# GpSimd's adaptive-norm sums in two runs around the mixer's last normalisation, its other small front work on VectorE, the second layer's gate in the later stage

## Chip, cores and metric

One NeuronCore of a Trainium2 chip runs the whole computation as one program. The metric is device time in microseconds (us); a run's time is that of one launch, and the number for a kernel is the median of several runs. The engines are named as in the profile: PE is TensorE (matrix products; PEld its weight load), DVE is VectorE, ACT is ScalarE, POOL is GpSimd, SP is SyncE, which here only starts transfers.

## What is computed

512 tokens of width 1024 go through two blocks. The parts that matter here, with the rest left out:

```python
def first_block(x, p, ...):
    h = x
    h = h + mixer(rms_norm(h, g_mix))              # conv of 3 and pooling of 2, 4, 8, 16, between w_in and w_o
    h = h + peer_ffn(rms_norm(h, g_ffn))           # 16 query projections, top 16 of 16384 experts a head
    gate = sigmoid(rms_norm(h, g_ple) @ w_ple_gate)
    h = h + gate * (p @ w_ple_proj)
    return rms_norm(h, g_final)

def second_block(x, c, ctx, c_ctx, ada_w, ada_b, ...):
    for i in range(2):                             # layer 0: window attention; layer 1: latent attention
        shift_x, scale_x, gate_x = split(silu(c) @ ada_w[i] + ada_b[i], 3)
        shift_c, scale_c, gate_c = split(silu(c_ctx) @ ada_w[i] + ada_b[i], 3)
        hx = rms_norm_2(x, norm_g[i]) * (1 + scale_x) + shift_x
        hc = rms_norm_2(ctx, norm_g[i]) * (1 + scale_c) + shift_c
        yx, yc = attention_i(hx, hc)
        x = x + gate_x * yx                        # ctx likewise in layer 0
    return rms_norm_2(x, final_g)
```

The product silu(c) @ ada_w[i] depends on no token. It can be done at any time before the layer that uses it.

## The kernel before

**Stages.** `mix` normalises the four token blocks (128 tokens each), turns them so that features lie on partitions, runs 16 projections of w_in (`proj`) in four groups of four, each with its pooling and its convolution, and then w_o as token-major products: two halves of 512 columns, four token blocks in each. As the second half of a token block is added to `h` (L367), that block's next norm is begun by `Norm.add`. `peer` then turns the normalised blocks (`flip`, L228) and runs 16 queries (`query`, L508 begins the evaluation of each product), each followed by one of 128 chunks of expert_u; after that come the routing (top-k, one-hot products) and the gathers of token block 0, on GpSimd's queue. `ple` computes the gate of the first block, `attn_a` and `attn_b` are the two layers of the second.

**A norm.** `rstat` squares a block on ScalarE (L111, summing along a row), then makes the factor `rn` in two tiny GpSimd operations on 128x1 (L112 and, with a power, L113). VectorE scales the rows with it at L217 (`xs`).

**Weights.** `unit` loads 512 KB (`raw`, three buffers, on SP's queue at L99), ScalarE rounds it into a high part (L93), and VectorE subtracts for the low part (L94, `wl`); each product is three matrix products (L104 to L106). Accumulators are three PSUM tiles (`acc`).

**Adaptive-norm sums.** `Ada.work` is a generator. One step takes 128 rows of ada_w by 512 columns (256 KB), multiplies by one column of `silu_c` per condition (x and context), and adds to `aacc`; eight such steps and one that stores make a half of a third (shift, scale or gate). On GpSimd one step is a load on its own queue (L783), a product (L794; L789 for the first) and a sum (L795) per condition. With `gpsimd=False` the step is one VectorE multiply-add per condition (L797) and a load on SP's queue (L785). Four thirds, (0,0), (0,1), (0,2) and (1,2) as (layer, third), are on GpSimd, (1,0) and (1,1) on VectorE beside `ple` and `attn_a`, where `later` takes two steps a time, 18 times.

**What sets the order.** Each engine executes its own list in order, and waits where an operand isn't there. The lists are made when the program is built: steps of `Ada.work` are drawn by `some(2)` at each projection and after each token block of w_o, then two a query, and a scheduler interleaves them with the rest. `issue_after(k.rs)` lets a load of a step be listed only behind the last norm factor that was written so far.

## Time and profile before

| | us |
|---|---|
| median of 3 runs | 2444.17 (2442.78 to 2445.14) |
| profiled execution | 2457.12 |
| its span | 2455.3 |
| PE busy | 2271.6 (93%) |
| DVE busy | 1858.9 (76%) |
| ACT busy | 1061.2 (43%) |
| POOL busy | 902.5 (37%) |

Busy times are means over stages with different limits, so they are read in stretches. A wait is put down to the operation that came last; the time of waiting in a list shows on the engine that waits, its cause on the engine that it waits for. The profiled execution is one execution, a little longer than the timed ones; durations come from it.

### The profile page before, as it was taken

The page shows a single profiled execution, that of the slowest core. Times are in us where ns is not written, and L with a number is a line of the kernel's source. Part 1 is how long each engine was busy: PE and PEld are TensorE (multiplying, and loading weights), DVE is VectorE, ACT ScalarE, POOL GpSimd, SP SyncE. Part 2 cuts the span into 40 slices and gives each one's busy share as a digit, 9 for nine tenths or more (in the row PEclk, how much of TensorE's full clock was granted, in tenths as well). Part 3 has the DMA queues.
Part 4 walks back from the last instruction along what each step waited for, and adds up shares of the span by engine and source line. Part 5 has one row for each costly group of instructions (what it writes and reads, how often), then busy time and mean ns, then how long its engine had stood idle before and what let it go on. Part 6 is the DMA issues. An engine that isn't in the chain of part 4 may idle for free. (4 is left out here: it accounts for less than half of the span.)

```text
span 2455.3 us, 35344 instructions
## 1 busy us (share of the span) xinstructions
PE 2271.6 (93%) x12631; PEld 1979.8 (81%) x12631; DVE 1858.9 (76%) x3421; ACT 1061.2 (43%) x1855; POOL 902.5 (37%) x1021
## 2 busy tenths in 40 slices
PE   7882999799999899999999999889999989999998
PEld 6661889799999899878888888568888758998886
DVE  8832788999999896888888874783688745378884
ACT  4212333243434343333333344441677623466772
POOL 8998920233232531423233210232233323023331
PEclk9985999899999999999999999999999989999999
DMA  5433543689989989999999975553201042210002
GB/s 192 141 120 104 176 139 123 207 286 335 351 311 356 359 321 333 376 377 388 381 372 364 364 268 160 174 177 105 69 31 34 9 148 89 84 46 27 27 10 95
DMA packets 187215, 492.64 MB, mean 201 GB/s; under 512 B 17294, under 2 KB 70814, under 8 KB 185504
## 3 DMA queue, kind: packets, MB, share of 16 engines
q1 hardware_dynamic: 127056, 265.94, 32.0%
q0 software_dynamic: 49040, 174.12, 19.9%
q10 hardware_dynamic: 10944, 50.34, 5.1%
q8 instruction: 99, 1.62, 0.3%
q14 instruction: 76, 0.62, 0.1%
HBM read 424.78 MB, written 65.55 MB: 200 GB/s over the span
## 5 line engine op out<-in xcount | busy, mean ns | idle before, releaser
L93 ACT ACTIVATE wh<-raw 128x1024 fp32r<-128x1024 f32 (+2 forms) x371 | 387.8, 1049 | 586.0 <-PE acc L105 175.8
L94 DVE TENSOR_TENSOR wl<-raw,wh 128x1024 fp32r<-128x1024 f32 (+2 forms) x371 | 465.4, 1259 | 138.3 <-ACT wh L93 133.0
L435 POOL DMA_INDIRECT grow<-in_expert_r,gidx x128 | 167.4, 1308 | 306.8 <-DVE gdot L448 276.1
L435 POOL DMA_INDIRECT grow<-in_expert_v,gidx x128 | 151.8, 1186 | 347.7 <-DVE h L460 329.8
L448 DVE CUSTOM_DVE_ANT_0 gjunk<-grow,gx 128x1024 bf16<-128x1024 f32 x128 | 156.0, 1219 | 17.2 <-DMA grow<-in_expert_r,gidx 16.7
L460 DVE SCALAR_TENSOR_TENSOR h<-grow,gdot,h 128x1024 f32<-128x1024 f32 x128 | 163.7, 1279 | 0.4
L945 DVE TENSOR_TENSOR ptl<-acc,pth 128x512 fp32r<-128x512 f32 x184 | 123.7, 686 | 30.2 <-ACT pth L944 28.6
L944 ACT ACTIVATE pth<-acc 128x512 fp32r<-128x512 f32 x184 | 106.2, 596 | 51.2 <-PE acc L1475 31.5
L1110 POOL TENSOR_SCALAR p<-p,st 128x256 f32<-128x256 f32 (+2 forms) x96 | 64.6, 674 | 136.9 <-DVE st L1109 97.9
L228 PE MATMUL tr<-ident,xs 128*128 128x128 f32 x220 | 46.3, 339 | 69.3 <-DVE xs L217 56.3
L1456 POOL TENSOR_SCALAR p<-p,st 128x768 f32<-128x768 f32 x64 | 60.3, 942 | 127.3 <-DVE st L1455 104.7
L228 PEld LDWEIGHTS tr<-ident,xs 128*128 128x128 f32 x220 | 32.4, 172 | 83.2 <-issue 31.2
L651 ACT ACTIVATE hs<-acc 128x384 f32<-128x384 f32 x128 | 61.3, 479 | 87.9 <-PE acc L106 87.4
L712 DVE TENSOR_TENSOR pr<-ht,gt 128x384 f32<-128x384 f32 x128 | 70.9, 557 | 15.5 <-DMA ht<-Hd 12.0
L106 PE MATMUL acc<-xn_0h,wl 128*128 128x384 f32 (+2 forms) x175 | 61.6, 352 | 19.7 <-DVE wl L94 19.7
L795 POOL TENSOR_TENSOR aacc<-aacc,araw 128x512 f32<-128x512 f32 x56 | 77.0, 1374 | 1.3
L620 PE MATMUL g<-oh,oh 128*128 128x128 f16 x768 | 56.8, 227 | 20.0 <-ACT gs L622 10.6
L1108 ACT ACTIVATE p<-S,st 128x257 f32<-128x257 f32 (+2 forms) x96 | 62.8, 655 | 25.8 <-DVE st L1106 14.7
L217 DVE TENSOR_SCALAR xs<-h,rn 128x1024 f32<-128x1024 f32 x16 | 12.5, 783 | 79.2 <-POOL rn L113 78.9
L620 PEld LDWEIGHTS <-oh 128*128 128x128 f16 x768 | 47.5, 101 | 29.1 <-issue 18.1
L104 PE MATMUL acc<-xn_0h,wh 128*128 128x384 f32 (+2 forms) x175 | 65.4, 374 | 4.2 <-DVE y L356 4.0
L613 DVE TENSOR_TENSOR oh<-oh,gb 128x1024 f16<-128x1024 f16 x96 | 61.8, 683 | 7.5 <-PE g L620 7.5
(1150 smaller groups left out, 7788.9 us busy)
## 6 DMA issues: line engine op xcount, KB each, us to landing
raw<-in_expert_u SPq DMA_DIRECT2D x128, 512.0 KB, 5.3
raw<-in_expert_v SPq DMA_DIRECT2D x128, 512.0 KB, 7.7
Hd<-hs ACTq DMA_DIRECT2D x64, 384.0 KB, 6.0
Gd<-gs ACTq DMA_DIRECT2D x12, 2048.0 KB, 11.6
gt<-Gd SPq DMA_DIRECT2D x32, 768.0 KB, 8.1
ht<-Hd SPq DMA_DIRECT2D x64, 384.0 KB, 8.8
araw<-in_ada_w POOLq DMA_DIRECT2D x64, 256.0 KB, 3.3
raw<-in_w_in SPq DMA_DIRECT2D x16, 512.0 KB, 3.5
```

What stands on the lines that cost most here:

```text
L93: nc.scalar.activation(hi[:, s], src[:, s], AF.Copy)
L94: self.wl = (sub or nc.vector).tensor_tensor(lo[:, s], src[:, s], hi[:, s].bitcast(F32), OP.subtract).ins
L104: mm(out, a[0], b[0], start=start, stop=False)
L228: k.nc.tensor.transpose(ps[:, i * P : (i + 1) * P], x[:, kc * P : (kc + 1) * P], k.ident)
L435: self.k.nc.gpsimd.indirect_dma_start(t, None, table, at)
L448: nc.vector.tensor_tensor_reduce(junk, t, self.x, 1.0, 0.0, OP.mult, OP.add, self.dot[:, s : s + 1])
L460: nc.vector.scalar_tensor_tensor(self.h, t, self.dot[:, s : s + 1], self.h, OP.mult, OP.add)
L620: nc.tensor.matmul(g[:, i], oh[2][at], oh[q][at], start=q == 0, stop=q == 1)
L712: nc.vector.tensor_tensor(by_g(pr), by_g(cur["h"][:, c % 2]), cur["g"][:, :, c % GC], OP.mult)
L795: nc.gpsimd.tensor_tensor(a, a, t, OP.add)
L944: k.nc.scalar.activation(hi, src, AF.Copy)
L945: (eng or k.nc.vector).tensor_tensor(lo, src, hi.bitcast(F32), OP.subtract)
```

## The change

GpSimd's thirds become (0,0), (0,1), (0,2). Their 54 steps are drawn in two runs. The first: each projection draws one or two steps in turn, 24 in all, and w_o draws none. Its loads may be listed once `mark` is written, a copy of one column of the first norm's last `xs`. The second run's 30 steps multiply by `silu_c2`, a copy of `silu_c` that VectorE makes behind the last L217 of the mixer (`resume`); two of them are drawn at each query. The third (1,2) goes to VectorE, and `later` takes three steps a time. The zeroing of the margins of `u` and `z`, two casts of the pooling's weights (L308, L309) and the four casts of indices in the routing (`sif`) go from GpSimd to VectorE. In the kernel after, lines stand one lower behind L72 (L112 becomes L113), L308 to L356 and L367 keep their numbers, and from `Ada` on they stand eight lower (L795 becomes L803).

```diff
@@ -71,6 +71,7 @@
         self.colt = col
         self.mhalf = self.cp.tile([P, 8], F32, name="mhalf")
         nc.gpsimd.memset(self.mhalf, -0.5)
+        self.mark = self.cp.tile([P, 1], F32, name="mark")
 
     def acc(self):
 
@@ -110,7 +111,7 @@
         nc = self.nc
         nc.scalar.activation(junk[:, :width], src, AF.Square, accum_out=out)
         nc.gpsimd.tensor_scalar(out, out, 1.0 / width, EPS, OP.mult, OP.add)
-        self.rs = nc.gpsimd.tensor_tensor(out, out, self.mhalf[:, :1], OP.pow).ins
+        nc.gpsimd.tensor_tensor(out, out, self.mhalf[:, :1], OP.pow)
 
     def norm_T(self, srcs, width, evac, bufs=5):
 
@@ -214,7 +215,7 @@
             src = x
             junk = sp.tile([P, w], BF16, tag="junk", name=k.nm("junk"), bufs=1)
         k.rstat(src, w, c, junk)
-        k.nc.vector.tensor_scalar(x, src, c, None, OP.mult)
+        k.normed = k.nc.vector.tensor_scalar(x, src, c, None, OP.mult).ins
         return x
 
     def flip(self, xs, evac):
@@ -276,7 +277,7 @@
     return [(src[first + i], kcs) for i in range(count)]
 
 
-def mix(k, h, x, ahead, work):
+def mix(k, h, x, ahead, ada, work):
 
 
     tc, nc, ap = k.tc, k.nc, k.ap
@@ -286,15 +287,14 @@
         mp = es.enter_context(tc.tile_pool(name="mx", bufs=1))
         yf = Feat(k, mp, 8, [(0, TB)], "my")
         unit = k.unit(ap["w_in"][12])
-        norm.flip([norm.add(t) for t in h], k.evac_gain(x, lambda kc: k.col("g_mix", kc)))
-
-        def some(n):
-            for _ in range(n):
-                next(work, None)
+        hn = [norm.add(t) for t in h]
+        k.begun = nc.gpsimd.tensor_copy(k.mark, hn[-1][:, 0:1]).ins
+        norm.flip(hn, k.evac_gain(x, lambda kc: k.col("g_mix", kc)))
 
         def proj(nb):
             uh, ul = unit if nb == 12 else k.unit(ap["w_in"][nb])
-            some(2)
+            for _ in range(1 + nb % 2):
+                next(work)
             return now(k.fm(x, 8, uh, ul, [0]))
 
         for g in range(4):
@@ -305,11 +305,11 @@
             if g == 0:
                 pwh, pwl = k.unit(ap["pool_w"], 512)
                 pwr = hilo(k, mp, [P, 512], "pwr")
-                nc.gpsimd.tensor_copy(pwr[0], pwh[:, 0:512].bitcast(F32))
-                nc.gpsimd.tensor_copy(pwr[1], pwl[:, 0:512].bitcast(F32))
+                nc.vector.tensor_copy(pwr[0], pwh[:, 0:512].bitcast(F32))
+                nc.vector.tensor_copy(pwr[1], pwl[:, 0:512].bitcast(F32))
                 pwh, pwl = pwr
-            nc.gpsimd.memset(u[:, :PAD], 0.0)
-            nc.gpsimd.memset(u[:, PAD + T :], 0.0)
+            nc.vector.memset(u[:, :PAD], 0.0)
+            nc.vector.memset(u[:, PAD + T :], 0.0)
             nc.scalar.activation(u[:, PAD : PAD + T], ps, AF.Copy)
             cur, lo, hi, s = u, 0, T + 2 * PAD, 1
             first = True
@@ -345,8 +345,8 @@
             nc.scalar.activation(c, psc, AF.Copy)
             psv = proj(8 + g)
             z = mp.tile([P, T + 2], F32, tag="z", name=k.nm("z"), bufs=2)
-            nc.gpsimd.memset(z[:, 0:1], 0.0)
-            nc.gpsimd.memset(z[:, T + 1 : T + 2], 0.0)
+            nc.vector.memset(z[:, 0:1], 0.0)
+            nc.vector.memset(z[:, T + 1 : T + 2], 0.0)
             nc.vector.tensor_tensor(z[:, 1 : T + 1], c, psv, OP.mult)
             y = mp.tile([P, T], F32, tag="y", name=k.nm("y"), bufs=2)
             nc.vector.tensor_scalar(y, z[:, 0:T], k.col("conv_w", g), None, OP.mult)
@@ -370,7 +370,8 @@
 
         ahead()
         units = [tm_units(ap["w_o"], 4 * nh, 2, 4) for nh in range(2)]
-        k.tm(yf, 8, units, range(TB), evac, between=8 * [lambda: some(2)])
+        k.tm(yf, 8, units, range(TB), evac)
+        ada.resume()
 
     return flips(k, norm, xs, x, "g_ffn"), xs
 
@@ -528,7 +529,7 @@
 
     def routing(tb):
         sif = rp.tile([P, 16, 16], BF16, tag="sif", name=k.nm("sif"), bufs=2)
-        nc.gpsimd.tensor_copy(sif, si[:, tb])
+        nc.vector.tensor_copy(sif, si[:, tb])
         cand = rp.tile([P, 8, 16, 16], F32, tag="cand", name=k.nm("cand"), bufs=1)
         svh = sv[:, tb].rearrange("p (h two) s -> p h two s", two=2)
         sih = sif.rearrange("p (h two) s -> p h two s", two=2)
@@ -757,11 +758,18 @@
         a = COLS["c"][0]
         self.s = k.cp.tile([P, 16], F32, name="silu_c")
         k.nc.scalar.activation(self.s, k.colt[:, a : a + 16], AF.Silu)
+        self.again = k.cp.tile([P, 16], F32, name="silu_c2")
         self.aff = k.cp.tile([P, 4, 16], F32, name="ada_aff")
         self.gate = k.dp.tile([3, D], F32, name="gate_d")
         self.parts = {
             (l, t, s): k.dp.tile([2, P, 512], F32, name=f"ada{l}{t}{s}") for l in range(2) for t in range(3) for s in range(2)
         }
+
+    def resume(self):
+
+        with self.k.tc.issue_after(self.k.normed):
+            self.k.nc.vector.tensor_copy(self.again, self.s)
+        self.s = self.again
 
     @staticmethod
     def conds(layer, third):
@@ -779,7 +787,7 @@
                 raw = pool.tile([P, 512], F32, tag="araw", name=k.nm("araw"), bufs=3)
                 w = k.ap["ada_w"][layer, kc, :, at : at + 512]
                 if gpsimd:
-                    with k.tc.issue_after(k.rs):
+                    with k.tc.issue_after(k.begun):
                         nc.gpsimd.dma_start(raw, w)
                 else:
                     nc.sync.dma_start(raw, w)
@@ -888,7 +896,7 @@
             before.pop(0)()
             ada.finish(0)
             apool = adx.enter_context(tc.tile_pool(name="adq", bufs=1, side="right"))
-            rest.append(ada.work(apool, [(1, 0), (1, 1)], False))
+            rest.append(ada.work(apool, [(1, 0), (1, 1), (1, 2)], False))
 
         def context():
             norm.append(Norm(k, D, 4, 3))
@@ -914,7 +922,7 @@
                 xs.append(norm[0].add(h[tb]))
 
         def later():
-            for _ in range(2):
+            for _ in range(3):
                 next(rest[0], None)
 
         units = [tm_units(ap["w_pg"], 4 * nh, 2, 4) for nh in range(2)]
@@ -1590,9 +1598,9 @@
         x2 = k.dp.tile([T, D], F32, name="x2d")
         x = Feat(k, xpool.enter_context(tc.tile_pool(name="xp", bufs=1)), 8, [(0, TB)], "xn")
         ada = Ada(k)
-        work = ada.work(adx.enter_context(tc.tile_pool(name="adp", bufs=1, side="right")), [(0, 0), (0, 1), (0, 2), (1, 2)], True)
+        work = ada.work(adx.enter_context(tc.tile_pool(name="adp", bufs=1, side="right")), [(0, 0), (0, 1), (0, 2)], True)
         qw = Query(k)
-        before, xs = mix(k, h, x, qw.load, work)
+        before, xs = mix(k, h, x, qw.load, ada, work)
         before, pT = peer(k, h, x, work, adx, qw, before, xs)
         xc = Feat(k, xpool.enter_context(tc.tile_pool(name="xcp", bufs=1)), 8, [(TB, 2)], "xc")
         before = ple(k, h, ada, adx, x, xc, x1, before, pT) + [hpool.close]
```

GpSimd's list at the first token block's norm factor in w_o, before (`rn` is the factor, `aacc`, `atmp` and `araw` belong to the steps):

```order
L795 TENSOR_TENSOR aacc252_1236<-aacc252_1236,araw254_1241 128x512
L795 TENSOR_TENSOR aacc251_1235<-aacc251_1235,atmp258_1276 128x512
L794 TENSOR_SCALAR araw257_1274<-araw257_1274,silu_c_106 128x512
L794 TENSOR_SCALAR atmp260_1283<-araw259_1281,silu_c_106 128x512
L795 TENSOR_TENSOR aacc252_1236<-aacc252_1236,araw257_1274 128x512
L795 TENSOR_TENSOR aacc251_1235<-aacc251_1235,atmp260_1283 128x512
L794 TENSOR_SCALAR araw259_1281<-araw259_1281,silu_c_106 128x512
L795 TENSOR_TENSOR aacc252_1236<-aacc252_1236,araw259_1281 128x512
L112 TENSOR_SCALAR rn274_1338<-rn274_1338 128x1
L113 TENSOR_TENSOR rn274_1338<-rn274_1338,mhalf_83 128x1
L783 DMA araw276_1344<-in_ada_w 128x512
L783 DMA araw278_1351<-in_ada_w 128x512
```

The same place after:

```order
L803 TENSOR_TENSOR aacc184_903<-aacc184_903,araw205_1008 128x512
L791 DMA araw308_1739<-in_ada_w 128x512
L113 TENSOR_SCALAR rn244_1241<-rn244_1241 128x1
L114 TENSOR_TENSOR rn244_1241<-rn244_1241,mhalf_83 128x1
L113 TENSOR_SCALAR rn247_1273<-rn247_1273 128x1
L114 TENSOR_TENSOR rn247_1273<-rn247_1273,mhalf_83 128x1
L113 TENSOR_SCALAR rn250_1305<-rn250_1305 128x1
L114 TENSOR_TENSOR rn250_1305<-rn250_1305,mhalf_83 128x1
L427 DMA grow255_1417<-in_row 128x1024
L113 TENSOR_SCALAR rn253_1337<-rn253_1337 128x1
L114 TENSOR_TENSOR rn253_1337<-rn253_1337,mhalf_83 128x1
L428 TENSOR_TENSOR gx_1413<-xs245_1242,grow255_1417 128x1024
```

Before, the four `rn` pairs stand between steps of third (0,2), with two steps drawn from one to the next; now the four stand in one piece behind the 24th step, and the steps behind `gx` read `silu_c2`.

VectorE's list in the mixer's first group, before (`ws` and `pooled` are the pooling, `wl` the low parts of weights):

```order
L94 TENSOR_TENSOR wl63_281<-raw61_278,wh62_280 128x512
L94 TENSOR_TENSOR wl72_306<-raw70_303,wh71_305 128x1024
L94 TENSOR_TENSOR wl81_353<-raw79_350,wh80_352 128x1024
L320 TENSOR_TENSOR ws66_291<-u54_239 128x527
L334 SCALAR_TENSOR_TENSOR pooled67_293<-ws66_291,u54_239 128x512
```

and after:

```order
L95 TENSOR_TENSOR wl61_277<-raw59_274,wh60_276 128x512
L308 CAST pwrh62_280<-wh60_276 128x512
L309 CAST pwrl63_281<-wl61_277 128x512
L95 TENSOR_TENSOR wl70_302<-raw68_299,wh69_301 128x1024
L320 TENSOR_TENSOR ws64_287<-u54_242 128x527
L95 TENSOR_TENSOR wl77_342<-raw75_339,wh76_341 128x1024
L334 SCALAR_TENSOR_TENSOR pooled65_289<-ws64_287,u54_242 128x512
```

The two casts now stand ahead of the weight splits of two projections.

VectorE's list at attn_a's last projections of a query, before (`qr` and `rope` are the rotary part of one block):

```order
L961 TENSOR_TENSOR qr2822_15021<-acc2821_14996,a_cs_14414 128x512
L966 TENSOR_TENSOR rope2823_15022<-acc2821_14996,a_cs_14414 128x16x16 x2
L961 TENSOR_TENSOR qr2827_15061<-acc2826_15036,a_cs_14414 128x512
L966 TENSOR_TENSOR rope2828_15062<-acc2826_15036,a_cs_14414 128x16x16 x2
L94 TENSOR_TENSOR wl2839_15119<-raw2837_15116,wh2838_15118 128x1024
L94 TENSOR_TENSOR wl2842_15125<-raw2840_15122,wh2841_15124 128x1024
L94 TENSOR_TENSOR wl2845_15131<-raw2843_15128,wh2844_15130 128x1024
```

and after:

```order
L805 SCALAR_TENSOR_TENSOR aacc2851_15190<-araw2859_15235,silu_c2_109,aacc2851_15190 128x512
L805 SCALAR_TENSOR_TENSOR aacc2851_15190<-araw2860_15238,silu_c2_109,aacc2851_15190 128x512
L969 TENSOR_TENSOR qr2821_15045<-acc2820_15020,a_cs_14372 128x512
L974 TENSOR_TENSOR rope2822_15046<-acc2820_15020,a_cs_14372 128x16x16 x2
L805 SCALAR_TENSOR_TENSOR aacc2851_15190<-araw2864_15273,silu_c2_109,aacc2851_15190 128x512
L805 SCALAR_TENSOR_TENSOR aacc2851_15190<-araw2865_15276,silu_c2_109,aacc2851_15190 128x512
L95 TENSOR_TENSOR wl2835_15106<-raw2833_15103,wh2834_15105 128x1024
L95 TENSOR_TENSOR wl2838_15112<-raw2836_15109,wh2837_15111 128x1024
L95 TENSOR_TENSOR wl2841_15118<-raw2839_15115,wh2840_15117 128x1024
L969 TENSOR_TENSOR qr2828_15087<-acc2827_15062,a_cs_14372 128x512
L974 TENSOR_TENSOR rope2829_15088<-acc2827_15062,a_cs_14372 128x16x16 x2
L95 TENSOR_TENSOR wl2844_15124<-raw2842_15121,wh2843_15123 128x1024
```

The last multiply-adds of the third (1,2) stand between the rotary blocks, ahead of the next weight splits; before, the last one stood ahead of these blocks.

SP's list at the same place, before:

```order
L785 DMA araw2861_15248<-in_ada_w 128x512
L99 DMA raw2804_14878<-in_a_qkv 128x1024
L99 DMA raw2837_15116<-in_a_qkv 128x1024
L99 DMA raw2840_15122<-in_a_qkv 128x1024
L785 DMA araw2865_15284<-in_ada_w 128x512
L99 DMA raw2843_15128<-in_a_qkv 128x1024
L99 DMA raw2846_15134<-in_a_qkv 128x1024
L99 DMA raw2872_15373<-in_a_g 128x1024
```

and after:

```order
L793 DMA araw2848_15158<-in_ada_w 128x512
L793 DMA araw2852_15191<-in_ada_w 128x512
L793 DMA araw2853_15194<-in_ada_w 128x512
L793 DMA araw2854_15197<-in_ada_w 128x512
L793 DMA araw2858_15232<-in_ada_w 128x512
L793 DMA araw2859_15235<-in_ada_w 128x512
L793 DMA araw2860_15238<-in_ada_w 128x512
L793 DMA araw2864_15273<-in_ada_w 128x512
L793 DMA araw2865_15276<-in_ada_w 128x512
L100 DMA raw2842_15121<-in_a_qkv 128x1024
L100 DMA raw2872_15363<-in_a_g 128x1024
L100 DMA raw2879_15449<-in_a_g 128x1024
```

The loads of the sums, 16 more in all and nine of them shown, now stand ahead of the last weight unit of a_qkv and of the units of a_g.

## Rows read from the trace of the kernel before

**Rows 1.** windows of 50 us: busy us of each engine (instructions), granted clock, DMA
```profile
200.00:250.00 50.00, 17.05 (x88) 15.44 (x88) 18.11 (x30) 14.42 (x27) 43.22 (x50) 0.55 0.33 105
250.00:300.00 50.00, 48.50 (x252) 42.66 (x253) 38.90 (x161) 17.59 (x28) 47.77 (x53) 1.00 0.55 179
...
350.00:400.00 50.00, 50.00 (x264) 44.52 (x263) 40.20 (x176) 18.86 (x31) 0.00 (x0) 1.00 0.37 121
```

**Rows 2.** waits of 0 to 400 us: us in total, times, longest
```profile
DVE xs L217 <- POOL rn L113: 73.7, 7, 44.4
...
PE tr L228 <- DVE xs L217: 51.4, 6, 29.6
...
DVE ws L320 <- POOL u L312: 7.9, 1, 7.9
```

**Rows 3.** timeline, VectorE: start, us, line, operation, [idle before <- releaser]
```profile
143.25 0.69 DVE L367 TENSOR_TENSOR h<-h,acc 128x512 f32<-128x512 f32 x1 [4.76 <-PE acc L106]
148.69 0.69 DVE L367 TENSOR_TENSOR h<-h,acc 128x512 f32<-128x512 f32 x1 [4.75 <-PE acc L106]
...
160.65 0.69 DVE L367 TENSOR_TENSOR h<-h,acc 128x512 f32<-128x512 f32 x1 [1.54 <-PE acc L106]
205.70 0.75 DVE L217 TENSOR_SCALAR xs<-h,rn 128x1024 f32<-128x1024 f32 x1 [44.37 <-POOL rn L113]
...
234.58 0.28 DVE L490 CAST iota<-cst 128x256 f16<-128x256 f32 x1
...
238.38 0.75 DVE L217 TENSOR_SCALAR xs<-h,rn 128x1024 f32<-128x1024 f32 x1 [2.17 <-POOL rn L113]
```

**Rows 4.** timeline, GpSimd
```profile
11.64 2.06 POOL L783 DMA_DIRECT2D araw<-in_ada_w  x3
...
143.91 1.30 POOL L795 TENSOR_TENSOR aacc<-aacc,araw 128x512 f32<-128x512 f32 x1
...
205.10 0.57 POOL L113 TENSOR_TENSOR rn<-rn,mhalf 128x1 f32<-128x1 f32 x1
...
235.72 1.71 POOL L789 TENSOR_SCALAR aacc<-araw,silu_c 128x512 f32<-128x512 f32 x2 [1.64 <-DMA araw<-in_ada_w]
...
279.35 0.59 POOL L800 DMA_DIRECT2D ada<-aacc  x1
```

**Rows 5.** timeline, ScalarE
```profile
161.37 1.06 ACT L111 ACTIVATE xs<-h 128x1024 f32<-128x1024 f32 x1 [4.00 <-DVE h L367]
...
249.33 0.60 ACT L508 ACTIVATE qh<-acc 128x512 fp32r<-128x512 f32 x1 [1.88 <-PE acc L106]
...
316.12 0.58 ACT L508 ACTIVATE qh<-acc 128x512 fp32r<-128x512 f32 x1
...
328.74 0.58 ACT L508 ACTIVATE qh<-acc 128x512 fp32r<-128x512 f32 x1
...
414.80 0.58 ACT L508 ACTIVATE qh<-acc 128x512 fp32r<-128x512 f32 x1
```

**Rows 6.** timeline, VectorE in the mixer
```profile
30.44 4.39 DVE L336 TENSOR_TENSOR pooled<-ws,cst 128x1 f32<-128x1 f32 x2
34.75 0.29 DVE L337 TENSOR_TENSOR pooled<-pooled,u 128x1 f32<-128x1 f32 x2
...
112.78 0.71 DVE L320 TENSOR_TENSOR ws<-u 128x527 f32<-128x527 f32 x1 [7.86 <-POOL u L312]
```

**Rows 7.** timeline, TensorE at the mixer's last group
```profile
122.41 0.80 PE L104 MATMUL acc<-ph,pwrh 128*128 128x512 f32 x1 [6.20 <-ACT c L345]
...
132.13 0.51 PE L104 MATMUL acc<-wh,my_3h 128*128 128x512 f32 x1 [3.66 <-ACT my_3h L944]
```

**Rows 8.** line L797: times, durations min/median/max in ns, first and last start
```profile
L797 DVE SCALAR_TENSOR_TENSOR aacc<-araw,silu_c,aacc x56: 733/745/1230, 1542.9 to 1655.8; 128x512 f32<-128x512 f32 x56
```

**Rows 9.** timeline, VectorE at attn_a's last projections
```profile
1665.02 0.69 DVE L961 TENSOR_TENSOR qr<-acc,a_cs 128x512 f32<-128x512 f32 x1 [8.50 <-PE acc L106]
...
1675.90 0.69 DVE L961 TENSOR_TENSOR qr<-acc,a_cs 128x512 f32<-128x512 f32 x1 [4.09 <-issue]
```

## The prediction

> **What bounds the kernel now.** I read the page first for where TensorE is idle. It is by far the busiest engine of the span (the table above) and has its worst place in the front, so I took the front in stretches of 50 us. In 200:250 TensorE works 17.05 us of 50 at a granted clock of 0.55, GpSimd works 43.22 us, and VectorE works 18.11; before and after that (250:300, 350:400) TensorE is full [rows 1]. So between the mixer and the queries TensorE waits, and GpSimd is the engine that is full. The list of waits names the reason: VectorE's row-scaling L217 waits 73.7 us for the norm factor `rn` that GpSimd makes at L113, 44.4 of it at once, and TensorE's transposes wait 51.4 us for L217 [rows 2].
>
> VectorE's own order shows how that closes into a chain. With nothing in its way it adds one token block of w_o each 5.44 us (143.25, 148.69). Block 0 gets its second half at 160.65; the norm factor comes only at 205.70, after 44.37 us idle. The three other blocks follow one by one (each needs its `rn`, and VectorE stands at L217 in between, so that TensorE's accumulators aren't emptied); the last L217 is at 238.38 [rows 3]. ScalarE had squared block 0 at 161.37 [rows 5], so GpSimd had its input from 162.6 on and made `rn` at 205.10 [rows 4]. In the order before, the two tiny `rn` operations stand behind the adaptive-norm steps. GpSimd was executing its list; 43 us of it stood in front.
>
> **The change part by part.** *The two runs.* GpSimd now has 24 steps (8 times 2, with a store step each, and 6) and then all four `rn` pairs in one piece; the next step reads `silu_c2`, which VectorE copies behind the last L217. What matters is whether GpSimd is through the 24 steps when block 0 is squared. Before, it starts them at 11.64, and the same 24 steps are done when the operation of 143.91 ends, at 145.2 [rows 4]: 5.56 us a step. First need is at 162.6. There are 17 us of margin; at this pace the wait at 205.70 goes wholly. What is late next: TensorE, whose blocks come every 5.44 us, and VectorE, which has three weight splits of a query between block 2 and block 3. Block 3 is done at 160.65 + 3 x 5.44 + 0.7 = 177.7, or 179.7 if the three splits (1.22 us each) stand in the way. Then ScalarE's square 1.06 and its read 0.19, GpSimd's pair about 0.9 with the gap, L217 0.75: the last L217 ends at 180.6 to 182.6, against 239.13 (238.38 + 0.75). That is **-56.5 to -58.5; I take -57**.
>
> From the last L217 to the first query's `qh` it takes 10.2 us now (239.13 to 249.33 [rows 5]), at a clock of 0.55 in this stretch. TensorE will have had no long idle time before it, so I take **-1.5** (0 to -3).
>
> *Memsets and casts to VectorE.* GpSimd's memset of `u` held VectorE for 7.86 us at 112.78 [rows 6], since it stood behind adaptive-norm work. Its group of pooling feeds the two waits of TensorE behind it, 6.20 and 3.66 [rows 7]. Without the wait VectorE goes on at once: **-7.9** (-6.2, the first wait alone, to -9.9, both). Against that stand two casts (128x512) and eight memsets in the mixer's loop, where VectorE has no idle time; the other eight stand at the start, where it waits for data. A cast of 128x256 took 0.28 at 234.58 [rows 3], so 0.56 for each of the two casts, and no VectorE memset is in the trace. Lower bound: the casts 1.1 and nothing for the memsets. Upper: in the mixer two 128x1 operations took 4.39 at 30.44, while two like them took 0.29 at 34.75 [rows 6], so 2.05 us is what one can lose beside GpSimd's work; if the casts and one memset in each of two groups lose that, it is 1.1 + 8.2, about 9. I take **+2.5**, the casts' own time and most of one such loss, nearer to the free price because the pair right behind the slow one lost nothing.
>
> The same rows are where a rule of the Trainium skill speaks against this part. The pair at 30.44 took 4.39 where 0.29 is the price [rows 6]. The Trainium skill (SBUF — State Buffer, section "Who interferes with whom") says that VectorE and GpSimd share one pair of ports as an exclusive lock, that copies and casts in their fast modes and operations with two SBUF inputs can be shut out for a whole instruction of the other, and that one with at most one SBUF input outside those modes can't. By that rule the memsets would cost VectorE their own time only, and each cast could lose one GpSimd operation (1.30 at 143.91 [rows 4]): an estimate by the page is +1.1 + 2.6, about +4, in place of my upper bound of 9. No run here shows a VectorE memset beside GpSimd, so the sum stays at +2.5 with the bounds above.
>
> *The second run in the query stage.* 30 steps start behind `gx`, about 4 us after the last L217, at 185. Their pace in that stage is read from a whole half-third between 235.72 and 279.35: 44 us for 9 steps, 4.9 each [rows 4]. They end at 185 + 147 = 332. The stage has 16 queries. While GpSimd worked, a query took 11.13 us (six from 249.33 to 316.12), and 10.76 without it (eight from 328.74 to 414.80) [rows 5]. Before, six or seven queries had GpSimd beside them; now about 13. Seven more at 0.37: **+2.5** (0, if the difference is TensorE's clock or transfers, to +6). The stage ends about 68 us earlier, at 358, and the routing's tiles that take the steps' memory are needed there, 26 us after the steps' end. So it costs nothing, but this is the margin to watch.
>
> *The four casts of routing.* 128x256 each, 0.28 by the row at 234.58 [rows 3], in a stage where VectorE is full: **+1** (0 to +2, reordering of its neighbours included).
>
> *Second layer's gate on VectorE.* 14 multiply-adds at 0.745 [rows 8] and two first products, 11.5 us, with 16 loads of 256 KB on SP's queue. The orders show that the first 56 multiply-adds keep their places and that the new ones stand between the rotary blocks of attn_a's last projections, ahead of three weight splits; the last weight unit of that projection now loads behind all 16 on SP. In this place VectorE is idle three times, 8.50 to 4.09 us, 16.7 in all [rows 9]. 11.5 fits into 16.7 if no load is late: **+1** (0 to +7: if half of the work falls outside the gaps and the splits come late). Behind it nobody waits for the gate until the second layer ends.
>
> Sum: -57 - 1.5 - 7.9 + 2.5 + 2.5 + 1 + 1 = **-59.4**. The profiled execution took 2457.12 (span 2455.3), so the same execution would take 2397.7. The median of the three runs, 2444.17, lies 12.95 under the profiled one; I carry that over: **2384.8**, rounded to 2385, 2.4% faster. With all best ends (-58.5, -3, -9.9, +1.1, 0, 0, 0) it is 2374; with all worst (-56.5, 0, -6.2, +9, +6, +2, +7) 2405.
>
> **The rivals.** *Given back in part.* The wait goes, but VectorE pays in its three full stretches: the mixer gains nothing (-7.9 + 9), the queries lose 6, the gate's work 7, the routing 2. -57 - 1.5 + 1 + 6 + 7 + 2 = -42.5: 2402. For it: the pair at 30.44, and VectorE full in the mixer. Against it: VectorE has 10 us in 50 free in the query stage [rows 1] and 16.7 in the place of the gate.
>
> *The first run is late.* Now all four factors stand behind 24 steps; if a step takes 6.8 us instead of 5.56, they end at 175 and block 0's factor comes 12 us late; the other three follow without a further wait. 2385 + 12 = 2397. Against it: two steps a projection or one and a half, GpSimd runs its list without pauses, and it loses 2 casts and 16 memsets.
>
> *Slower: the second run holds the routing.* All 30 steps now fall into the query stage, next to VectorE, and the routing's first tiles can't start before the steps' memory is free. It decides from 5.8 us a step on (run's end at 358 instead of 332); each further microsecond of a step costs 30 us, and at 7.8 the gain is gone. If VectorE's use of the shared memory path stretched a step to 8.6, the run would end at 443, 85 us past the need: 2385 + 85 = 2470. For it: the pair at 30.44 shows that one of these two engines can hold the other up by a whole operation [rows 6]. Against it: 4.9 is a mean over a stretch with just this company [rows 4].
>
> *It doesn't do what it says* would need GpSimd to pass a step of the second run before the last norm; the orders show none, and I give that nothing.
>
> **How the numbers follow.** Forecast (2385, own range 2374 to 2395) 0.68; given back in part (2395 to 2410, likeliest 2402) 0.22; first run late (2397) 0.06; second run holds the routing 0.04, of which 0.03 above the old time. A measurement of this kernel can tell about 0.2%, 5 us, from no change. So faster 0.96, same 0.01, slower 0.03. The range 2373 to 2404 holds the forecast, the late first run and over half of the give-back.
>
> **What would show it.** In the profile of the changed kernel: (1) the wait of L218 (the old L217) for GpSimd's L114 is under 3 us in sum outside the first norm, and the last L218 of the mixer starts at about 180 minus the mixer's 5 us; (2) GpSimd is idle from about 143 to the first `rn`; (3) TensorE's clock has no stretch at 0.55 between mixer and queries; (4) ws at L320 doesn't wait for GpSimd, and TensorE's wait behind c is gone; (5) the queries are 11.1 us apart until about 330; (6) VectorE's gaps in attn_a are filled and TensorE has no new wait over 2 us there. Wrong I would be if GpSimd's second run ended behind the last query, if the casts held TensorE's first projections for more than a few microseconds, or if the peer stage, whose order on VectorE is reshuffled by the scheduler, gave away what the front had gained.

## The result, and the profile after

The changed kernel takes 2385.24 us in the median of four runs (2381.87 to 2392.25), the kernel before 2444.65 in four runs beside them (2442.78 to 2446.61): a ratio of 0.9759, with a 95% interval of 0.9741 to 0.9778. That is 59.4 us less; 2385 was forecast. The profiled execution of after took 2381.87 (span 2379.9), 3.4 under its median, while that of before lay 12.5 over its own, so the two traces differ by 75 us and not by 59. Most of the other 16 are placed below, under the sum.

The stretches in which TensorE stood still ([rows 1]) are gone. These are the windows of after, with the same columns; queries now begin at 176:

```profile
100.00:150.00 50.00, 46.80 (x198) 37.71 (x198) 29.99 (x34) 11.90 (x15) 35.26 (x37) 0.97 0.51 163
150.00:200.00 50.00, 48.05 (x268) 41.88 (x267) 34.26 (x104) 22.97 (x41) 29.72 (x35) 1.00 0.35 119
200.00:250.00 50.00, 46.79 (x237) 41.12 (x236) 40.33 (x152) 15.70 (x27) 46.81 (x49) 0.97 0.52 167
...
300.00:350.00 50.00, 49.88 (x265) 44.58 (x264) 39.91 (x159) 18.07 (x29) 8.57 (x8) 1.00 0.40 132
```

GpSimd is still at its first run in a part of 100:150. In 150:200 TensorE works 48.05 us of 50 at a granted clock of 1.00; in the stretch 200:250 of before it was 17.05 at 0.55. The list of waits of after, to be read beside [rows 2]:

```profile
DVE xs L218 <- POOL rn L114: 13.2, 6, 6.7
...
PE tr L229 <- DVE xs L218: 1.3, 3, 0.8
```

VectorE's 73.7 us at the row scaling are 13.2, of which 8.1 stand in the first norm. TensorE's transposes wait 1.3 us for it in place of 51.4. VectorE's timeline of after, beside [rows 3] and [rows 6]:

```profile
20.97 3.42 DVE L308 CAST pwrh<-wh 128x512 fp32r<-128x512 f32 x1
24.30 0.41 DVE L309 CAST pwrl<-wl 128x512 fp32r<-128x512 f32 x1
...
45.22 0.06 DVE L348 MEMSET z<- 128x1 f32 x1
...
105.02 1.79 DVE L320 TENSOR_TENSOR ws<-u 128x527 f32<-128x527 f32 x1
...
148.12 0.69 DVE L367 TENSOR_TENSOR h<-h,acc 128x512 f32<-128x512 f32 x1 [1.52 <-PE acc L107]
151.01 0.75 DVE L218 TENSOR_SCALAR xs<-h,rn 128x1024 f32<-128x1024 f32 x1 [2.20 <-POOL rn L114]
...
156.44 0.75 DVE L218 TENSOR_SCALAR xs<-h,rn 128x1024 f32<-128x1024 f32 x1 [2.19 <-POOL rn L114]
...
161.88 0.75 DVE L218 TENSOR_SCALAR xs<-h,rn 128x1024 f32<-128x1024 f32 x1 [2.19 <-ACT wh L94]
162.54 3.49 DVE L95 TENSOR_TENSOR wl<-raw,wh 128x1024 fp32r<-128x1024 f32 x3
165.95 0.68 DVE L367 TENSOR_TENSOR h<-h,acc 128x512 f32<-128x512 f32 x1
...
168.83 0.75 DVE L218 TENSOR_SCALAR xs<-h,rn 128x1024 f32<-128x1024 f32 x1 [0.63 <-POOL rn L114]
```

Block 0 has its second half at 148.12, the four scalings start 2.2, 2.2, 2.2 and 0.6 us after VectorE has come to them, and the last ends at 169.58. A memset (`z` at 45.22) takes 0.06 and starts before the operation ahead of it has ended; the first cast takes 3.42, the second 0.41. GpSimd's timeline, beside [rows 4]:

```profile
137.13 1.31 POOL L803 TENSOR_TENSOR aacc<-aacc,araw 128x512 f32<-128x512 f32 x1
...
150.15 0.18 POOL L113 TENSOR_SCALAR rn<-rn 128x1 f32<-128x1 f32 x1 [10.86 <-ACT xs L112]
150.42 0.56 POOL L114 TENSOR_TENSOR rn<-rn,mhalf 128x1 f32<-128x1 f32 x1
155.59 0.19 POOL L113 TENSOR_SCALAR rn<-rn 128x1 f32<-128x1 f32 x1 [4.61 <-ACT xs L112]
...
308.33 0.56 POOL L808 DMA_DIRECT2D ada<-aacc  x1 [0.30 <-POOL aacc L803]
392.46 3.98 POOL L436 DMA_INDIRECT grow<-in_expert_r,gidx  x1 [83.56 <-DVE gidx L441]
```

The first run's last sum ends at 138.4. GpSimd waits 10.86 us for ScalarE and then serves each block at once. The second run's last store goes out at 308.33, and 84 us later the first gather. ScalarE's `qh`, beside [rows 5]:

```profile
176.26 0.60 ACT L509 ACTIVATE qh<-acc 128x512 fp32r<-128x512 f32 x1 [1.80 <-PE acc L107]
...
313.79 0.58 ACT L509 ACTIVATE qh<-acc 128x512 fp32r<-128x512 f32 x1
```

### The profile page after: what moved, and what is told of

Its sections match the earlier page's. It is cut to its first block, busy times and chain, and to the rows that moved or that the text cites. A ratio compares the mean times of both kernels' runs of the same rounds, so it can differ in the third digit from the quotient of the medians.

```text
span 2379.9 us, 35348 instructions
## 1 busy us (share of the span) xinstructions
PE 2256.2 (95%) x12631; PEld 1967.5 (83%) x12631; DVE 1867.3 (78%) x3460; ACT 1062.0 (45%) x1855; POOL 849.8 (36%) x954
## 5 line engine op out<-in xcount | busy, mean ns | idle before, releaser
L94 ACT ACTIVATE wh<-raw 128x1024 fp32r<-128x1024 f32 (+2 forms) x371 | 388.3, 1050 | 563.8 <-PE acc L106 172.5
L803 POOL TENSOR_TENSOR aacc<-aacc,atmp 128x512 f32<-128x512 f32 x42 | 64.7, 1540 | 1.2
L1460 DVE TENSOR_REDUCE st<-S 128x1 f32<-128x768 f32 x64 | 60.8, 951 | 4.9 <-PE S L107 4.2
L1114 DVE TENSOR_REDUCE st<-S 128x1 f32<-128x257 f32 (+2 forms) x96 | 61.6, 643 | 3.5
L1462 ACT ACTIVATE p<-S,st 128x768 f32<-128x768 f32 x64 | 57.4, 897 | 8.7 <-DVE st L1460 8.0
```

Of the source, the lines that this page charges most:

```text
L94: nc.scalar.activation(hi[:, s], src[:, s], AF.Copy)
L1462: nc.scalar.activation(p, S[:, :NT], AF.Exp, bias=st[:, 0:1], accum_out=st[:, 1:2])
```

## The experiments

Each kernel was timed against the kernel before on the same chip; 2446.4, 2450.4 and 2449.3 were its medians for the three sets. Two kernels of different sets are best compared by their ratios. All kernels give TensorE the same products, in the same order but for neighbours that are a place apart, so the start of the n-th product shows where in the program time comes and goes. I read these from the traces (us; 500 lies in w_o's first half, 700 just ahead of the first `qh`, 1600 at the end of the last query, 5600 in the sums over expert_v, 7600 and 8400 on both sides of attn_a's projections):

```
product no.            500    700   1600    5600    7600    8400    last
before               148.5  248.7  423.9  1118.2  1580.4  1745.3  2443.3
after                136.9  176.1  355.0  1039.7  1502.1  1673.1  2369.6
after, second trace  140.5  179.9  363.8  1050.2  1512.3  1684.8  2377.9
runs alone           142.4  181.6  372.3  1059.9  1521.6  1686.3  2380.5
small work alone     132.7  246.8  422.5  1110.5  1572.8  1738.5  2431.2
gate alone           149.2  248.0  421.1  1109.7  1571.7  1744.6  2435.1
after, no small work 143.0  182.1  361.9  1050.5  1512.7  1682.7  2374.5
after, no gate       140.2  179.4  362.1  1054.7  1516.0  1682.4  2375.4
after, no hold       140.1  279.3  451.1  1138.6  1600.5  1772.1  2466.6
after, all late      123.5  162.7  345.5  1090.0  1551.7  1721.3  2416.0
sixteen, direct      128.1  167.3  352.5  1038.2  1500.4  1671.8  2368.2
```

**The two runs alone.** The small work and the gate stay on GpSimd. The edit is shown against the kernel after; the other memsets, the casts, and the two steps a call of the later stage go back likewise.

```diff
-            nc.vector.memset(u[:, :PAD], 0.0)
+            nc.gpsimd.memset(u[:, :PAD], 0.0)
...
-work = ada.work(..., [(0, 0), (0, 1), (0, 2)], True)
+work = ada.work(..., [(0, 0), (0, 1), (0, 2), (1, 2)], True)
```

> Only the two runs: the steps are drawn 1, 2, 1, 2 a projection, none in w_o, and the second run is held by the copy behind the last L217; memsets, casts and the gate (1,2) stay on GpSimd, so the second run has 48 steps. Theory (the wait for the norm factor behind GpSimd's list is the whole matter, 57 us): 2444 - 57 - 1.5 + 3 = about 2389, the four factors come within 2 us of their squares; the second run ends at about 175 + 134 + 18 x 2.45 = 353, just ahead of the last query's end. Rival (the second run holds the routing when the gate stays on GpSimd): its end falls behind the last query and the time is 2400 or more. Rival (the gain came from the small work): over 2430.

Measured: 2394.19, ratio 0.9784 (0.9765 to 0.9802). The runs alone bring 52 of the 59 us. Between the products 1200 and 1400 they take 49.4 us, where the two traces of after take 38.7 and 42.8, and not by holding the routing: the run ends at 359, and the first `sif` on GpSimd starts at 373. In VectorE's timeline of this kernel, and GpSimd's of the same microseconds:

```profile
283.56 10.76 DVE L95 TENSOR_TENSOR wl<-raw,wh 128x1024 fp32r<-128x1024 f32 x1
294.25 0.08 DVE L528 MATCH_VALUE_LOAD si<-sv,s 128x8 f32 x1
```

```profile
283.68 1.30 POOL L803 TENSOR_TENSOR aacc<-aacc,atmp 128x512 f32<-128x512 f32 x1
284.94 0.70 POOL L802 TENSOR_SCALAR araw<-araw,silu_c 128x512 f32<-128x512 f32 x1
285.61 0.69 POOL L802 TENSOR_SCALAR atmp<-araw,silu_c 128x512 f32<-128x512 f32 x1
...
292.56 0.68 POOL L802 TENSOR_SCALAR araw<-araw,silu_c 128x512 f32<-128x512 f32 x1
293.20 0.58 POOL L791 DMA_DIRECT2D araw<-in_ada_w  x1
293.81 1.63 POOL L803 TENSOR_TENSOR aacc<-aacc,araw 128x512 f32<-128x512 f32 x1
```

One weight split of 1.22 us takes 10.76, while GpSimd executes ten operations without a gap. It ends 1.1 us after GpSimd goes to issue a transfer at 293.20. TensorE then waits 8.85 us for the next `ql`.

**The small work alone**, on the kernel before.

```diff
-            nc.gpsimd.memset(u[:, :PAD], 0.0)
+            nc.vector.memset(u[:, :PAD], 0.0)
```

and likewise the margins of `z`, the casts at L308 and L309 and `sif`.

> Only the small work moves: the memsets of u and z, the two casts of the pooling's weights and the four casts of sif go to VectorE; the adaptive-norm steps are drawn as before. Theory (GpSimd's list sets when the norm factor comes, so what the mixer gains is lost again in the wait at L217): the mixer's tail is 5 to 10 us earlier, the wait at L217 longer by as much, 2444 less about 3 (the casts and memsets that GpSimd no longer does): 2441. Rival (terms add up whatever else is there): 5 to 10 us less, 2434 to 2439.

Measured: 2445.07, ratio 0.9993 (0.9978 to 1.0008): no change. Product 500 comes 15.8 us earlier, product 700 only 1.9: the wait at L217 grew from 44.37 to 58.45, as this kernel's VectorE shows.

```profile
204.94 0.75 DVE L217 TENSOR_SCALAR xs<-h,rn 128x1024 f32<-128x1024 f32 x1 [58.45 <-POOL rn L113]
```

So GpSimd's list sets when the factor comes, whatever the mixer gains.

**The gate alone**, on the kernel before.

```diff
-rest.append(ada.work(apool, [(1, 0), (1, 1)], False))
+rest.append(ada.work(apool, [(1, 0), (1, 1), (1, 2)], False))
...
-            for _ in range(2):
+            for _ in range(3):
                 next(rest[0], None)
```

(1,2) is taken from GpSimd's list as well.

> Only the gate (1,2) moves: 18 steps less on GpSimd at the end of its run beside the queries, 14 multiply-adds and two products more on VectorE, three steps a call. Theory (the splits of attn_a's last projection come late, 4 us in the trace of after, and the queries gain about 1.5): 2444 + 2.5 = 2447. Rival (hidden in VectorE's idle time): 2442 to 2443.

Measured: 2454.74, ratio 1.0039 (1.0024 to 1.0053): slower by 0.4%, more than either theory had. From product 7600 to 8400 this kernel takes 172.9 us; the kernels with the gate on GpSimd (before, runs alone, small work alone, no gate) take 164.7 to 166.4, those with it on VectorE 169.6 to 172.9. In the mean the gate costs 6 us there, 3 to 8 by single traces. The trace of this kernel is of its fastest execution (2447.13), so what makes up the rest of the 8 us between the medians isn't shown.

**After without the small work.**

```diff
-            nc.vector.memset(z[:, 0:1], 0.0)
+            nc.gpsimd.memset(z[:, 0:1], 0.0)
```

and the other moved memsets and casts likewise.

> The changed kernel with the memsets, the two casts and the sif casts back on GpSimd. Theory (the small work is worth what the mixer gained in the two traces, 10 to 12 us): 2385 + 8 to 11 = 2393 to 2396, with VectorE's wait for u of about 8 us back. By the forecast's term (-7.9 + 2.5 + 1 = -4.4): 2389. Rival (the casts on VectorE cost what the memsets gain): 2385.

Measured: 2388.10, ratio 0.9772 (0.9752 to 0.9792): 2.9 more than after, within the intervals. The wait for `u` did not come back; one for `z` did, in VectorE's timeline at the mixer's last group:

```profile
99.69 1.79 DVE L320 TENSOR_TENSOR ws<-u 128x527 f32<-128x527 f32 x1
...
117.58 1.55 DVE L352 TENSOR_SCALAR y<-z,col 128x512 f32<-128x512 f32 x1 [5.67 <-POOL z L349]
```

**After without the gate** (the third (1,2) back on GpSimd, two steps a call).

```diff
-rest.append(ada.work(apool, [(1, 0), (1, 1), (1, 2)], False))
+rest.append(ada.work(apool, [(1, 0), (1, 1)], False))
```

> The changed kernel with the gate (1,2) back on GpSimd behind the second run (48 steps) and two steps a call in the later stage. Theory (the gate on VectorE costs 5 to 8 us in attn_a, where the trace of after shows TensorE's place slip by 6): 2385 - 6 = 2379, the second run ends near 350, before the last query's tiles are needed. Rival (as in the kernel with the runs only: a VectorE weight split shut out for 10 us by GpSimd in the query stage, or the run holds the routing): 2388 to 2395.

Measured: 2386.69, ratio 0.9740 (0.9722 to 0.9759): no difference from after that the intervals show. attn_a's 5 to 6 us come back, and the second run, which now ends at 366, holds the routing: from product 1600 to 1800 it takes 5.5 us more than after, and VectorE waits for the run's last store:

```profile
368.19 0.29 DVE L532 CAST sif<-si 128x256 bf16<-128x256 uint32 x1 [4.88 <-DMA ada<-aacc]
```

**After without the hold.**

```diff
         with self.k.tc.issue_after(self.k.normed):
             self.k.nc.vector.tensor_copy(self.again, self.s)
-        self.s = self.again
```

> The changed kernel without the hold: the second run's steps read silu_c and not its copy made behind the last L218, all else as it is. The scheduler then lists nearly all 30 steps of the second run ahead of the first of the four norm factors. Theory (GpSimd's list is the cause of the wait): the first factor comes at about 139 + 28 x 4.6 = 268, the other three at once behind it, the last L218 at 280 instead of 169, the queries without GpSimd beside them: 2385 + 110 - 5 = about 2490, slower than before. Rival (the hold is not needed, the places where steps are drawn keep the order): 2385.

Measured: 2475.44, ratio 1.0096 (1.0079 to 1.0113): slower than before. The scheduler lists the second run ahead of the factors, and VectorE waits 100 us for the first one, then 3.64 and less:

```profile
253.48 1.75 DVE L218 TENSOR_SCALAR xs<-h,rn 128x1024 f32<-128x1024 f32 x1 [100.00 <-POOL rn L114]
...
259.46 0.75 DVE L218 TENSOR_SCALAR xs<-h,rn 128x1024 f32<-128x1024 f32 x1 [3.64 <-POOL rn L114]
...
269.97 2.85 DVE L218 TENSOR_SCALAR xs<-h,rn 128x1024 f32<-128x1024 f32 x1 [0.64 <-POOL rn L114]
```

Against after the last scaling comes 103 us later, and the time is 90 us longer by the medians, 82 by the ratios. Seven are won back in the queries, which then take 171.8 us from product 700 to 1600 without GpSimd beside them.

**The pooling's weights split straight into their tiles**, gate on GpSimd.

```diff
-                pwh, pwl = k.unit(ap["pool_w"], 512)
-                pwr = hilo(k, mp, [P, 512], "pwr")
-                nc.vector.tensor_copy(pwr[0], pwh[:, 0:512].bitcast(F32))
-                nc.vector.tensor_copy(pwr[1], pwl[:, 0:512].bitcast(F32))
-                pwh, pwl = pwr
+                raw = k.wp.tile([P, 1024], F32, tag="raw", name=k.nm("raw"), bufs=3)
+                nc.sync.dma_start(raw[:, :512], ap["pool_w"])
+                pwh, pwl = hilo(k, mp, [P, 512], "pwr")
+                put_split(k, pwh, pwl, raw[:, :512])
```

> The changed kernel with the gate back on GpSimd, and the pooling's weights split straight into their tiles, without the two casts. Theory (the cast of 3.42 us beside GpSimd cost the first projections 3 to 5 us, the gate 6): 2385 - 6 - 3 = 2376. Rival (what is won in the mixer's start is lost against VectorE later in the mixer, and the gate's place brings nothing): 2383 to 2390.

Measured: 2387.36, ratio 0.9745 (0.9719 to 0.9772): nothing over the kernel without the gate. Without the casts product 100 comes 2 to 3 us earlier than in the two traces of after, but now a weight split at 21.5 is held up, 4.21 us in place of 1.22.

**All steps late.** The projections draw no step.

```diff
-            for _ in range(1 + nb % 2):
-                next(work)
```

> The changed kernel with no first run: the projections draw no step, all 54 come behind the last L218. Tests the rival that a long second run holds the routing. Theory of that rival: the mixer is 5 to 15 us shorter without GpSimd beside VectorE; the run starts near 165 and ends at 165 + 54 x 4.5 = 408, while the routing needs the memory at about 345 and the first gather stands behind it: 2385 - 10 + 60 = about 2435. If the routing doesn't wait for the run: 2375.

Measured: 2428.94, ratio 0.9915 (0.9898 to 0.9931). It is the rival of the long second run, made real. The mixer is 13.4 us shorter (product 500), and the routing's first operation waits 59.40 us for the run's last store; here in VectorE's timeline and the windows:

```profile
407.23 0.29 DVE L530 CAST sif<-si 128x256 bf16<-128x256 uint32 x1 [59.40 <-DMA ada<-aacc]
```

```profile
300.00:350.00 50.00, 49.81 (x266) 44.98 (x265) 40.99 (x159) 17.24 (x27) 45.86 (x44) 1.00 0.53 169
350.00:400.00 50.00, 7.85 (x46) 7.53 (x44) 0.00 (x0) 1.92 (x4) 48.42 (x57) 0.61 0.26 83
```

The rival's mechanism is real, then, and this change only stays clear of it. The loss, 44 us by the medians, is the wait of 59 less what the mixer gained.

**The late thirds in another order.**

```diff
-[(1, 0), (1, 1), (1, 2)], False
+[(1, 2), (1, 0), (1, 1)], False
```

> The changed kernel with the three late thirds in another order on VectorE: (1,2) first, then (1,0) and (1,1). The same operations; in the tail beside attn_a's last projections each load then feeds two multiply-adds, and 13 loads instead of 16 stand ahead of the last weight unit. Theory (VectorE's late splits there come from multiply-adds that wait for their loads, one load each): 2385 - 2 = 2383, with the slip of 4 us at that place gone in part. Rival (it is the work, not the loads): 2385 to 2388.

Measured: 2389.68, ratio 0.9747 (0.9727 to 0.9768), beside 2390.13 for after on the same chip: no difference. Its stretch from product 7600 to 8400 takes 168.1 us against 171.0 and 172.5 of after; if that is worth anything, it is too little to see in the time. The slip that the theory aimed at did not go: from product 8000 to 8050 TensorE takes 17.0 us here, 16.4 and 17.2 in the two traces of after, 12.4 before. In this place VectorE waits once for a load (1.58 us at 1588.03) and once for a store of the sums (3.30 at 1598.32), and then no more; yet the three splits start 4 us after the first of them could (1610.24), behind multiply-adds that run without a wait:

```profile
1607.45 5.09 DVE L805 SCALAR_TENSOR_TENSOR aacc<-araw,silu_c,aacc 128x512 f32<-128x512 f32 x6
...
1614.38 3.48 DVE L95 TENSOR_TENSOR wl<-raw,wh 128x1024 fp32r<-128x1024 f32 x3
```

**One step a projection**: 16 in the first run, 38 in the second; alone, and with the direct split.

```diff
-            for _ in range(1 + nb % 2):
-                next(work)
+            next(work)
```

> The changed kernel with one step drawn a projection: 16 in the first run, 38 in the second. Theory (the first run costs the mixer 13.4 us through VectorE, as the kernel without it showed, so a third of it gives 4.5 back; the second run ends at 172 + 38 x 4.45 = 341, just ahead of the need at about 345; three more queries have GpSimd beside them, +1): 2385 - 3.5 = 2381.5. Rival (what GpSimd takes from VectorE in the mixer it takes in the query stage, or the longer run holds the routing): 2385 to 2390.

> As the kernel with one step drawn a projection, and the pooling's weights split straight into their tiles, without the two casts. Theory: 2381.5 - 1.5 = 2380, with TensorE's first projections 3 us earlier. Rival (the mixer's early gain is lost to VectorE later): the same as with the casts.

> The changed kernel itself, for its time on the same chip as the three others and for a second trace: 2385 by all; the places that differ between its two traces show how far one execution differs from the next (by the kernels so far, 5 to 10 us in the gathers' stage).

Measured on one chip: after 2390.13, ratio 0.9754 (0.9736 to 0.9772); sixteen steps 2385.22, 0.9734 (0.9710 to 0.9757), not to be told from it; sixteen and the direct split 2380.40, 0.9720 (0.9707 to 0.9733), 0.4% under after with intervals that don't overlap. The kernel with sixteen and the direct split is the fastest of the study. Its window at the mixer's end shows GpSimd nearly idle and TensorE full, to be read beside 100:150 of after above:

```profile
100.00:150.00 50.00, 49.74 (x218) 40.57 (x217) 24.79 (x33) 11.49 (x15) 4.07 (x7) 1.00 0.31 106
```

Its second run ends at 338, ahead of the need.

## Why the prediction was right, step by step

**The wait for the norm factor: -57, and it was -57.0.** From block 0's second half to the end of the last scaling it took 78.5 us (160.65 to 239.13) and takes 21.5 (148.12 to 169.58). The cause is shown, not argued: undoing the hold alone puts 100 us of wait back, and gains ahead of that wait vanish in it (small work alone). Blocks come each 5.44 us; the three weight splits ahead of block 3 cost 1.5 of the 2 us that were left open (block 2 at 159.00, block 3 at 165.95).

**From the last scaling to `qh`: -1.5, measured -3.5** (10.2 to 6.7), a little outside its bounds of -3 to 0. TensorE had half of the transposes done before the last scaling ended. The granted clock in these microseconds was 0.70 before, not the 0.55 that the prediction took from the row of 50 us, and is 1.00 after.

**The mixer: -5.4 forecast; -12.5 in the trace (160.65 to 148.12), -8 at product 500 in the second one.** The mechanism was the one that was named: the 7.86 us for `u` are gone, and TensorE's wait of 6.20 behind `c` with them. The term was mis-sized; its best bounds together (-9.9 + 1.1 = -8.8) don't hold the first trace. For one part, small work alone, on the kernel before, brings product 500 forward by 15.8. For another, which I had not counted, with fewer steps drawn in the mixer the memsets come earlier even on GpSimd (in runs alone VectorE waits 5.4 us for `z`, and not for `u`), and runs alone gains 6. The two don't add up to what after gains there (11.6 and 8.0), and what makes up the 15.8 isn't shown. In the whole time the small work shows 2.9 on the kernel after and 1.3 on the kernel before, neither clear of the noise, so its term of -7.9 + 2.5 + 1 = -4.4 is neither borne out nor refuted. The two casts took 3.42 and 0.41, 3.8 together, inside the bounds of 1.1 to 9; the eight memsets in the loop took 0.06 to 0.07 each, also those of `z` at 45.22 and 70.81, where GpSimd was executing a sum or a product. Here the rule of the Trainium skill (SBUF — State Buffer, section "Who interferes with whom") and the trace agree on what is held up: no memset was, a cast was. They differ on how long: the estimate by the page had a cast lose one GpSimd operation of 1.30, and the first cast lost 3.0.

**The queries: +2.5, measured +3.7 and +8.7** in the two traces of after (175.2 us from product 700 to 1600 before, 178.9 and 183.9 after). The pace was 11.46 us a query to 313.79, not 11.13: GpSimd beside VectorE is dearer than the six queries of before showed. The second run ended at 309, 23 us earlier than forecast: it started 10 earlier (174.81 and not 185), and a step took 4.5 us and not 4.9. The rival that it holds the routing was far off in this kernel, and is real in the two with a longer run.

**The routing's casts: +1.** Each takes 0.29 us on VectorE. From product 1600 to 1800, where the first two stand, after takes 39.4 and 39.8 us and before 39.2: inside the bounds of 0 to +2.

**The gate: +1, measured 6 in the mean.** This term was mis-sized; the step that failed is "11.5 fits into 16.7 if no load is late". The loads were late, and the work stood in front of the splits. VectorE's rows of after at this place, and ScalarE's next weight unit in after and in before:

```profile
1598.48 1.22 DVE L805 SCALAR_TENSOR_TENSOR aacc<-araw,silu_c,aacc 128x512 f32<-128x512 f32 x1 [0.48 <-DMA araw<-in_ada_w]
1601.74 1.54 DVE L805 SCALAR_TENSOR_TENSOR aacc<-araw,silu_c,aacc 128x512 f32<-128x512 f32 x2 [2.05 <-DMA araw<-in_ada_w]
...
1604.46 2.41 DVE L805 SCALAR_TENSOR_TENSOR aacc<-araw,silu_c,aacc 128x512 f32<-128x512 f32 x2
1606.79 3.48 DVE L95 TENSOR_TENSOR wl<-raw,wh 128x1024 fp32r<-128x1024 f32 x3
```

```profile
1611.92 1.06 ACT L94 ACTIVATE wh<-raw 128x1024 fp32r<-128x1024 f32 x1 [7.17 <-DMA raw<-in_a_qkv]
```

```profile
1683.88 1.06 ACT L93 ACTIVATE wh<-raw 128x1024 fp32r<-128x1024 f32 x1 [2.89 <-DMA raw<-in_a_qkv]
```

Five of these multiply-adds wait 0.5 to 2 us for their loads (5.0 us in all), and the last four stand ahead of the three splits, which start 4.7 us late against the rest of the program (1606.79; 1602.1 would be the time of before less 76.2). Their buffer comes free later, and the last weight unit of a_qkv is loaded 4 us later: ScalarE waits 7.17 us for it in place of 2.89. TensorE's products slip by 4.0 there. Late loads are not the whole of it: in the kernel with the late thirds in another order one load is late, by 1.58, and the slip is as large. How much is the loads and how much the work's place in VectorE's list stays open. The upper bound, +7, held the cost; the value that I took didn't.

**The sum.** Two terms came out better than forecast by about 5 to 9 us, two worse by 6 to 11. That 2385 was met to the microsecond is luck in this part; that the time falls by some 57 and not by 20 is not. Carrying the 12.95 us from the profiled execution over to the median was sound: the trace of before is slow by some 6 us from product 1600 to 5600 (694.3 us; the other traces of the table take 684.7 to 692.6, but for the kernel with all steps late) and by 1.5 to 7.5 behind 8400, where the change does nothing.

**The signs.** Right: GpSimd idle from 139 to 150, no clock at 0.55, no wait for `u`, VectorE's gaps in attn_a filled. Wrong: the waits for the factor are 5 us in sum outside the first norm, not under 3, because each block pays ScalarE's square and GpSimd's two operations while VectorE stands; the last scaling at 168.83, where about 175 was forecast, since the mixer is shorter; the pace of the queries; and TensorE's slip in attn_a.

## What to carry to other kernels

When one engine's list holds both bulk work and a tiny operation that others wait for, look first at what stands ahead of the tiny one; moving the bulk away is worth the whole wait, and nothing saved ahead of the wait counts until then. Placing the steps elsewhere in the program text didn't order them; something that they read did (the copy made behind the norm). Work that is moved into another engine's idle time fits only if its loads are there by then and it stands in the list where the idle time is, not ahead of what others wait for.

## What the runs showed of the hardware that I had not expected

A VectorE operation with two inputs can be shut out for as long as GpSimd runs without a gap: 10.76 us for one of 1.22, through ten GpSimd operations, let in when GpSimd went to issue a transfer. It needs no transfer to be let in: the first cast of after, begun at 20.97, ended at 24.39, having lost 3.0 us through three GpSimd operations, and the fourth took 1.20 where such a product takes 0.69 elsewhere. The third and fourth:

```profile
22.74 1.25 POOL L803 TENSOR_TENSOR aacc<-aacc,atmp 128x512 f32<-128x512 f32 x1
23.98 1.20 POOL L802 TENSOR_SCALAR araw<-araw,silu_c 128x512 f32<-128x512 f32 x1
```

In other places weight splits lose 1 to 4 us at a time, not the same ones from one execution to the next (3.38 at 308.20 in the second trace of after, none there in the first). How much this comes to can be read by adding up what VectorE's weight splits of 128x1024 took above 1.22 us. Up to product 500 it is 7.6 us in after, and 0.1 in the kernel with all steps late, which has no GpSimd step there. From product 700 to 1600 it is 10.8 and 14.1 in the two traces of after, 22.6 in runs alone, and 0.1 in the kernel without the hold, where GpSimd is idle. Of the 9 us by which the two traces of after differ at product 1600 (3.8 up to product 700, 5 in the queries), the splits lose 5.4; what makes up the rest isn't shown.
